# One paired comparison for both one-hots of the gate matrices, and the routing's selection product moved to VectorE

## Chip, core and metric

The kernel runs on one core of a Trainium2 chip. The metric is the device time of one execution in microseconds (us); less is better. The kernel before took 4143.04 us in the median of three runs (4133.16 to 4143.84).

## What is computed

Two trunk layers over 768 tokens of width 1024 (512 latent, 256 context), in float32. Layer 0 mixes tokens by a state-space scan, layer 1 by latent attention. After each mixer comes a PEER channel mixer, and the change lies in it alone:

```python
def peer_route(t, w_q, keys):                      # 8 heads, 128 keys a side, 16 kept
    q = (t @ w_q).reshape(n_tok, 8, 2, 64)
    s = einsum('thsd,hsnd->thsn', q, keys)
    sv, si = lax.top_k(s, 16)                      # per side: scores and key numbers
    cand = sv[:, :, 0, :, None] + sv[:, :, 1, None, :]
    cv, ci = lax.top_k(cand.reshape(n_tok, 8, 256), 16)
    i1 = take_along_axis(si[:, :, 0], ci // 16, -1)
    i2 = take_along_axis(si[:, :, 1], ci % 16, -1)
    return i1 * 128 + i2, softmax(cv)              # 128 experts a token of 16384, their gates

def peer_channel(h, ...):
    act = gelu(einsum('td,tkd->tk', hb, u_tab[ib])) * gb
    return einsum('tk,tkd->td', act, v_tab[ib])
```

## The kernel before, in words

**Tiles of tokens.** Six tiles of 128 tokens: 0 and 1 are context, 2 to 5 latent. In layer 0 tiles 2 to 5 are dense (every one of the 16384 experts is computed for them, and a token's gates, spread over all experts, are zero where an expert was not chosen) and tiles 0 and 1 are gathered (their experts' rows are fetched one by one by indirect DMA). In layer 1, which needs the latent tokens only, tiles 4, 2, 3 are dense and tile 5 is gathered.

**Routing** (`route`, L958, ten tiles in all: six in layer 0, four in layer 1). PE multiplies queries by keys (L984), ACT copies the scores (L987), and VectorE finds the 16 best per head and side (`top16`, L970 to L976), then the 16 best sums (L1010), then the gates (L1014 to L1019) and the positions a and b of the two halves (L1024 to L1034). The key numbers are picked by a selection product: L1039 compares 0..15 with the position into `oh`, 128x2048 in bf16, on VectorE, once per side; L1041 multiplies it by the key numbers `sib` on GpSimd; L1044 (three halvings) and L1045 add it up on VectorE into `rt`.

**Gate matrices** (`gate_matrix`, L1056, seven dense tiles in all). PE turns `rt` (L1064), ACT copies it to `iT` (L1066) and keeps a negated copy (L1067). Then come 16 steps of eight tokens, the one-hots three steps (`GA`) ahead of the products. In `one_hots`, VectorE compares 0..127 with the second keys of eight tokens at once (L1077, `o2`, 128x1024 in f32); `o1`, the one-hot of the first key times the gate, is made token by token: five of eight on VectorE (L1083, comparison and product in one instruction), three of eight (`NACT`) on ACT by two ACTIVATEs each (L1087 and L1088). In `products`, PE makes eight 128x128 float32 products (L1099) and ACT moves four of them at a time from PSUM into `stage` (L1101), whose writes hop by 32 elements. After four steps ACT's queue stores `stage`, 2 MB, to DRAM (L1103). There are 112 such steps, 64 in layer 0 and 48 in layer 1.

**Dense experts.** `dense_u` (L1134) multiplies tokens by 128 experts' u rows with weights split in two float32r parts (split at L305 on ACT and L306 on VectorE or GpSimd). The first 40 blocks of 128 in layer 0 and 48 in layer 1 are made ahead of the gates (`ahead`, L1140, their split on GpSimd) and parked in DRAM. `dense` (L1156) loads the gates `Gt` (on SP's queue, behind the last store of gates), multiplies, and accumulates over v rows (L1204). `gather` (L1257) runs beside: GpSimd issues the row fetches (L1272), VectorE makes the dot products (L1279) and sums (L1284).

**What sets the order.** `merge` emits several streams side by side by a clock of expected times; in `peer` (L1315) the gate matrices and the blocks ahead are the main streams and the gathering is at the side. Then a scheduler orders each engine's instructions by readiness in its own model of costs and hands out buffers. Twenty 4 KB slots (`N4`) per partition are shared by `o1`, `o2`, `oh`, the parts of u and others; `c5` slots are 512 bytes.

Of the kernel before, what the change touches and what calls it, by code (L numbers as in the profile page):

```python
# [35 lines left out]
# Slots of SBUF, by size, that all phases share.  # L36
# [4 lines left out]
NACT = 3  # L41
# [23 lines left out]
def merge(*streams, side=()):  # L65
    """Emits generators side by side; each yields the time its last step takes, or is expected to take. Ends with the
    first ones; those at the side can go on later."""
    clocks = [[0.0, n, s, n < len(streams)] for n, s in enumerate(streams + tuple(side))]
    while any(c[3] for c in clocks):
        c = min(clocks, key=lambda c: (c[0], c[1]))  # L70
        try:
            c[0] += next(c[2])
        except StopIteration:
            clocks.remove(c)
# [12 lines left out]
def pipeline(steps, ahead):  # L87
    """Emits (prepare, work) pairs, with the preparations so many steps ahead of the work."""
    got = []
    for n in range(len(steps) + ahead):  # L90
        if n < len(steps):
            got.append(steps[n][0]())
        if n >= ahead:
            yield steps[n - ahead][1](got[n - ahead])
            got[n - ahead] = None
# [12 lines left out]
class Net:  # L108
    def __init__(self, ctx, tc, a, out, dbg=None):
# [9 lines left out]
        self.iota128 = self.sb.tile([128, 128], F32, name="iota128")  # L119
# [9 lines left out]
    def phase(self, name):  # L129
        """The 48 KB that each phase cuts up as it needs."""  # L130
        self.phases.close()
        self.pool = self.phases.enter_context(self.tc.tile_pool(name=name, bufs=1, reuse_waits="tile"))
# [53 lines left out]
    def ada(self, l, q):  # L186
        """Modulation vectors 2q and 2q+1 of layer l: rows to DRAM, columns to modT."""
# [39 lines left out]
    def adas(self, lqs):  # L227
        """The modulation vectors of several (layer, q); the last part of each runs some steps behind."""
# [12 lines left out]
    def rstd(self, var, eps):  # L241
        """1/sqrt(var + eps) for a [128, 1] operand, with one Newton step."""
# [36 lines left out]
    def transpose_to(self, dst, src, nblk):  # L279
        """dst [128, nblk, 128] <- src [128, nblk*128] transposed by 128-column blocks."""  # L280
# [8 lines left out]
    def mod_transpose(self, h, l, s, i):  # L289
        """[128, 8, 128] <- (h * (1 + mod i+1) + mod i) transposed."""  # L290
# [12 lines left out]
    def split(self, hi, lo, x, lo_eng):  # L303
        """x = hi + lo exactly, both in float32r."""
# [27 lines left out]
    def sin_acc(self, out, x, shift):  # L332
        """sin(x + shift), shift 0 or pi/2, with the argument reduced to [-pi, pi]."""
# [15 lines left out]
    def s5_params(self):  # L349
        """Powers 0..8 of the discrete poles, f * B, and the 8th powers in the scan's layout."""  # L350
        nc, a, par = self.nc, self.a, self.par
        V, GP = nc.vector, nc.gpsimd
        # State before each chunk, [chunk, re/im, (direction, group pair)].
# [4 lines left out]
        # Selects one group of a pair, for both halves of the partitions.  # L358
# [17 lines left out]
        # c of both groups of a pair, by direction, with zeros for the other group's states.  # L376
# [53 lines left out]
        # The 8th and 16th powers as products need them: [state's part, result's part, (direction, group pair)].  # L430
# [15 lines left out]
        # The powers 1..8 again, for both groups of a pair, on both halves of the partitions.  # L446
# [17 lines left out]
    def s5_input(self):  # L464
        """Modulates u, [(j, c), g, chunk], in place."""
# [19 lines left out]
    def s5_advance(self, E, to, of, n, dg, nd):  # L485
        """Adds a step of eight tokens from chunk `of` to chunk `to`, and n - 1 times again for every second chunk on, for nd
        (direction, group pair) from dg."""
# [12 lines left out]
    def s5_prep(self):  # L500
        """Per batch of four (direction, group pair): the chunks' inputs to the states, lag kernels."""
# [7 lines left out]
        def krons(b):  # L509
            """Q, whose rows j are f B times the powers 7 - j forward, j backward."""  # L510
# [14 lines left out]
        def turn(b, Q):  # L525
# [10 lines left out]
            # Lag kernels of both groups of the pairs.  # L536
# [63 lines left out]
    def s5_mout(self):  # L600
        """What the states add to the outputs, [(re/im, state), direction and group pair, group of the pair, (j, c)]:
        rows j are c times the powers j + 1 forward, 8 - j backward."""
# [28 lines left out]
    def s5_scan(self):  # L631
        """The states, [(group of the pair, state), chunk, re/im, direction and group pair], in place; chunks that are done
        are turned to [(re/im, state), chunk, group of the pair, ...]."""
# [26 lines left out]
    def s5_fill(self, fb):  # L660
        """The states between, of four group pairs, both directions; then turned to [(re/im, state), chunk, group of the
        pair, ...]."""
# [10 lines left out]
    def s5_readout(self, mout):  # L673
        """gelu(y + d u), transposed: yc [128, 4, 256] x 2 for the context, yl [128, 2, 512] x 4."""
# [60 lines left out]
    def load_w(self, src, name, n=D):  # L735
        """[D, n] weight as eight tiles [128, n]."""
# [7 lines left out]
    def y_tile(self, ti, k):  # L744
        """Feature block k of tile ti's s5 output, transposed."""
# [5 lines left out]
    def glu(self, ti, wg):  # L751
        """y <- y * sigmoid(y w), in place."""
# [18 lines left out]
    def out_steps(self, l, pair, src, parts, first, rows):  # L771
        """Steps of h <- LN(ALPHA h + m2 * (y w)) for two tiles; parts() gives y's two parts, transposed, as four tiles
        [128, part, block, token]."""
# [134 lines left out]
    def query_steps(self, l, pair, H):  # L908
        """Steps to the PEER layer's input of two tiles, transposed, in two parts, in H; for gathered ones in rows; and to
        the queries, transposed."""  # L910
# [47 lines left out]
    def route(self, ti):  # L958
        """Routes one tile of 128 tokens: its gates and experts, spread over all experts (dense) or listed."""
# [32 lines left out]
        sib = self.c5([128, 2, 8, 16], "sib", BF16)  # L992
        V.tensor_copy(out=sib, in_=si)
        # Candidate pairs (a, b) in the order of 16 a + b, of which those with (a + 1)(b + 1) > 16 can't be among the 16
        # best: row 0 whole, eight of each of rows 1 to 7, the first of rows 8 to 15.
# [16 lines left out]
        # gates  # L1012
# [7 lines left out]
        # position -> (a, b)  # L1020
# [17 lines left out]
        for s in range(2):  # L1038
            V.tensor_tensor(out=oh[s], in0=self.iota16.unsqueeze(1).to_broadcast(full),  # L1039
                            in1=ab[:, s, :].rearrange("p (h k) -> p h k", h=8).unsqueeze(2).to_broadcast(full), op=ALU.is_equal)  # L1040
            GP.tensor_tensor(out=oh[s], in0=oh[s], in1=sib[:, s].unsqueeze(3).to_broadcast(full), op=ALU.mult)  # L1041
        for s in range(2):
# [13 lines left out]
    def gate_matrix(self, ti, n_act=NACT):  # L1056
        """Writes tile di's gates, spread over all experts, to DRAM: [i1 / 8, i2, tile, token / 32, i1 % 8, token % 32]."""
# [7 lines left out]
        iT = self.t2([128, 4, 128], "iT")  # L1065
        S.copy(out=iT[:, 0:3], in_=tp)  # L1066
        S.mul(out=iT[:, 3], in_=tp[:, 0], mul=-1.0)  # L1067
# [3 lines left out]
        def one_hots(q):  # L1071
            """Of eight tokens: the second keys, and the first ones times the gates."""
            t0 = q * 8
            ts = slice(t0, t0 + 8)
            sh = [128, 8, 128]
            o2 = self.t4(sh, "o2")
            V.tensor_tensor(out=o2, in0=self.iota128.unsqueeze(1).to_broadcast(sh),  # L1077
                            in1=iT[:, 1, ts].unsqueeze(2).to_broadcast(sh), op=ALU.is_equal)
            o1 = self.t4(sh, "o1")
            nv = 8 - n_act  # L1080
            for t in range(nv):
                E = GP if t < NPOOL else V
                E.tensor_scalar(out=o1[:, t, :], in0=self.iota128, scalar1=iT[:, 0, t0 + t:t0 + t + 1],  # L1083
                                scalar2=iT[:, 2, t0 + t:t0 + t + 1], op0=ALU.is_equal, op1=ALU.mult)
            for t in range(nv, 8):
                c = t0 + t
                S.activation(out=o1[:, t, :], in_=self.iota128, func=AF.Abs, bias=iT[:, 3, c:c + 1])  # L1087
                S.activation(out=o1[:, t, :], in_=o1[:, t, :], func=AF.Relu, scale=-2.0, bias=iT[:, 2, c:c + 1])  # L1088
            return o1, o2

        def products(q, o):
# [4 lines left out]
            for t4 in range(2):  # L1096
# [4 lines left out]
                S.copy(out=stage[:, :, c:c + 4].rearrange("p i t -> p t i"), in_=gp)  # L1101
# [7 lines left out]
    def gate_matrices(self, n_tiles):  # L1109
        """Of all dense tiles, once the queries of so many tiles are there."""  # L1110
# [14 lines left out]
    def dense_u(self, Us):  # L1125
        """gelu(h u) of 128 experts, [expert, token]."""
# [13 lines left out]
    def ahead(self, l, n, n_tiles):  # L1140
        """The first n blocks' gelu(h u), to DRAM, for use when the gates are there."""
# [14 lines left out]
    def dense(self, l):  # L1156
        """All experts for the tokens of the dense tiles, in blocks of 128 experts; eight blocks to an accumulation."""
# [61 lines left out]
        def work_tile(d):  # L1219
            """The second half of one tile's last accumulation."""  # L1220
# [36 lines left out]
    def gather(self, l, row_time):  # L1257
        """The experts of the other tiles' tokens, row by row."""
# [43 lines left out]
    def peer_out(self, l, ti, f, rows=None):  # L1302
        """h <- LN(ALPHA h + m5 f)."""
# [30 lines left out]
    def mla(self, dense, gather):  # L1334
# [96 lines left out]
        def project(h):  # L1431
            if h % 2 == 0:
# [10 lines left out]
                # Each head's two parts, the first where the head was, the second on the other half of the partitions.  # L1443
# [21 lines left out]
        def scores(h, qi):  # L1465
            """Softmax of one head's scores for 128 queries."""
# [86 lines left out]
def layouts(inputs):  # L1553
    """The inputs as the kernel reads them: copies, transposes and slices only, and tables of shapes alone."""
# [65 lines left out]
```

## Time and profile before

| | us |
|---|---|
| median of three runs | 4143.04 |
| all three | 4143.84, 4143.04, 4133.16 |
| time of the profiled execution | 4133.16 |
| its span | 4133.2 |
| PE busy in it | 3683.9 |
| DVE (VectorE) busy | 3320.3 |
| ACT (ScalarE) busy | 1661.6 |
| POOL (GpSimd) busy | 1716.7 |

The profiled execution is the fastest of the three; its span is its whole time, and the median lies 9.9 us above it. Busy times are sums of one engine's instructions, idle time taken out. A share over the whole span mixes the stages: it is read by stretches below.

### The profile page before, as it was taken

The page shows a single profiled execution, that of the slowest core. Times are in us where ns is not written, and L with a number is a line of the kernel's source. Part 1 is how long each engine was busy: PE and PEld are TensorE (multiplying, and loading weights), DVE is VectorE, ACT ScalarE, POOL GpSimd, SP SyncE. Part 2 cuts the span into 40 slices and gives each one's busy share as a digit, 9 for nine tenths or more (in the row PEclk, how much of TensorE's full clock was granted, in tenths as well). Part 3 has the DMA queues.
Part 4 walks back from the last instruction along what each step waited for, and adds up shares of the span by engine and source line. Part 5 has one row for each costly group of instructions (what it writes and reads, how often), then busy time and mean ns, then how long its engine had stood idle before and what let it go on. Part 6 is the DMA issues. An engine that isn't in the chain of part 4 may idle for free. (4 is left out here: it accounts for less than half of the span.)

```text
span 4133.2 us, 54988 instructions
## 1 busy us (share of the span) xinstructions
PE 3683.9 (89%) x18795; PEld 3040.0 (74%) x18795; DVE 3320.3 (80%) x6733; ACT 1661.6 (40%) x3133; POOL 1716.7 (42%) x1160
## 2 busy tenths in 40 slices
PE   6758968688789999999999989988778899999998
PEld 3437857577667788778888855568778678989997
DVE  9884497999967788988889844468999678888887
ACT  2222335368922232233333233354579333333333
POOL 5834257345422455555555300056445113333341
PEclk7879989899999999999999999999889999999999
DMA  5556234258898799999999820144358878897976
GB/s 180 152 170 228 84 112 148 74 194 273 282 344 301 278 340 344 339 347 340 332 339 346 321 101 3 44 158 134 122 192 271 308 268 316 294 337 278 346 287 219
DMA packets 398457, 986.21 MB, mean 239 GB/s; under 512 B 67040, under 2 KB 147424, under 8 KB 393568
## 3 DMA queue, kind: packets, MB, share of 16 engines
q1 hardware_dynamic: 217120, 501.34, 34.8%
q0 software_dynamic: 110592, 402.70, 27.6%
q10 hardware_dynamic: 70464, 78.65, 5.6%
q8 instruction: 148, 2.42, 0.2%
q14 instruction: 133, 1.09, 0.1%
HBM read 892.28 MB, written 90.21 MB: 238 GB/s over the span
## 5 line engine op out<-in xcount | busy, mean ns | idle before, releaser
L1204 PE MATMUL acc<-Ws,A 128*128 128x512 f32 x5208 | 1204.4, 392 | 54.0 <-ACT A L305 26.5
L1134 PE MATMUL s_ps<-Hs,Uh 128*128 128x512 f32 (+1 forms) x4096 | 1188.9, 371 | 9.6 <-ACT Uh L305 8.7
L1204 PEld LDWEIGHTS acc<-Ws,A 128*128 128x128 f32 x5208 | 982.6, 189 | 271.5 <-DVE Ws L306 35.7
L1272 POOL DMA_INDIRECT row<-in_peer_u,idx x384 | 515.2, 1342 | 823.7 <-DVE row L1279 688.6
L1134 PEld LDWEIGHTS s_ps<-Hs,Uh 128*128 128x128 f32 x4096 | 764.2, 191 | 104.0 <-ACT Uh L305 9.8
L1134 PE MATMUL s_ps<-Hs,Ul 128*128 128x512 f32 (+1 forms) x2048 | 760.7, 371 | 55.8 <-POOL Ul L306 55.7
L1272 POOL DMA_INDIRECT row<-in_peer_v,idx x384 | 479.8, 1250 | 553.8 <-DVE f L1284 489.3
L1284 DVE SCALAR_TENSOR_TENSOR f<-row,act,f 128x1024 f32<-128x1024 f32 x381 | 487.7, 1280 | 39.1 <-DMA row<-in_peer_v,idx 37.7
L1279 DVE SCALAR_TENSOR_TENSOR row<-row,m 128x1024 f32<-128x1024 f32 x384 | 467.1, 1234 | 47.7 <-DMA row<-in_peer_u,idx 46.7
L305 ACT CAST Ws<-W 128x512 fp32r<-128x512 f32 x512 | 306.0, 619 | 495.8 <-DMA W<-in_peer_v 437.0
L1134 PEld LDWEIGHTS s_ps<-Hs,Ul 128*128 128x128 f32 x2048 | 390.4, 191 | 109.3 <-POOL Ul L306 62.6
L306 DVE TENSOR_TENSOR Ws<-W,Ws 128x512 fp32r<-128x512 f32 x512 | 346.2, 686 | 107.8 <-ACT Ws L305 107.3
L305 ACT CAST Uh<-U 128x1024 fp32r<-128x1024 f32 x256 | 268.7, 1052 | 317.9 <-DMA U<-in_peer_uT 257.5
L1137 ACT ACTIVATE ge<-s_ps 128x512 f32<-128x512 f32 (+1 forms) x256 | 139.5, 545 | 454.2 <-PE s_ps L1134 415.9
L306 POOL TENSOR_TENSOR Ul<-U,Uh 128x1024 fp32r<-128x1024 f32 x88 | 228.3, 2596 | 217.0 <-ACT Uh L305 193.8
L1099 PE MATMUL g_ps<-o,o 128*128 128x128 f32 x1792 | 236.0, 289 | 89.6 <-DVE o L1083 75.5
L1099 PEld LDWEIGHTS g_ps<-o,o 128*128 128x128 f32 x1792 | 226.0, 201 | 100.5 <-DVE o L1083 34.1
L306 POOL TENSOR_TENSOR Wos<-wo,Wos 128x512 fp32r<-128x512 f32 x60 | 87.5, 1484 | 472.3 <-PE tp_ps L286 351.2
L305 ACT CAST A<-ge 128x512 fp32r<-128x512 f32 (+1 forms) x256 | 144.6, 565 | 294.7 <-DVE ge L1185 290.5
L1101 ACT COPY stage<-g_ps 128x512 f32<-128x512 f32 x224 | 229.2, 1091 | 55.6 <-PE g_ps L1099 55.1
L306 DVE TENSOR_TENSOR Ul<-U,Uh 128x1024 fp32r<-128x1024 f32 x168 | 205.1, 1221 | 42.2 <-ACT Uh L305 41.4
L1185 DVE TENSOR_TENSOR ge<-ge,Gt 128x512 f32<-128x512 f32 (+1 forms) x256 | 155.9, 620 | 78.1 <-ACT ge L1137 50.6
(346 smaller groups left out, 4927.3 us busy)
## 6 DMA issues: line engine op xcount, KB each, us to landing
U<-in_peer_uT SPq DMA_DIRECT2D x256, 512.0 KB
W<-in_peer_v SPq DMA_DIRECT2D x512, 256.0 KB
gm<-stage ACTq DMA_DIRECT2D x28, 2048.0 KB
ada_wt<-in_ada_w SPq DMA_DIRECT2D x96, 512.0 KB
Gt<-gm SPq DMA_DIRECT2D x16, 2048.0 KB
Gt<-gm SPq DMA_DIRECT2D x16, 1536.0 KB
wq<-in_peer_w_q SPq DMA_DIRECT2D x40, 512.0 KB
wo<-in_s_w_o SPq DMA_DIRECT2D x48, 256.0 KB
```

The costliest lines, as they stand in the source:

```text
L305: self.nc.scalar.copy(out=hi, in_=x)
L306: lo_eng.tensor_tensor(out=lo, in0=x, in1=hi.bitcast(F32), op=ALU.subtract)
L1099: PE.matmul(out=gp[:, t, :], lhsT=o[1][:, t4 * 4 + t, :], rhs=o[0][:, t4 * 4 + t, :], start=True, stop=True)
L1101: S.copy(out=stage[:, :, c:c + 4].rearrange("p i t -> p t i"), in_=gp)
L1134: PE.matmul(out=sp, lhsT=x[:, k, :], rhs=self.Hs[:, y, k, :], start=(n == 0), stop=(n == 3 * KD - 1))
L1137: S.activation(out=ge, in_=sp, func=AF.Gelu)
L1185: V.tensor_tensor(out=gv, in0=gv, in1=Gt[b // SB][:, :, :, b % SB, :], op=ALU.mult)
L1204: PE.matmul(out=acc[hf][d], lhsT=A[b][:, x, c], rhs=Ws[:, y], start=(j == 0 and n == 0), stop=(j == SB - 1 and n == 2))
L1272: GP.indirect_dma_start(out=r, out_offset=None, in_=tab, in_offset=bass.IndirectOffsetOnAxis(ap=ik[:, k:k + 1], axis=0), element_offset=l ...
L1279: x = V.scalar_tensor_tensor(out=r, in0=r, scalar=1.0, in1=m, op0=ALU.mult, op1=ALU.mult, accum_out=act[:, k:k + 1])
L1284: x = V.scalar_tensor_tensor(out=f, in0=r, scalar=act[:, k:k + 1], in1=f, op0=ALU.mult, op1=ALU.add)
```

## The change

`iota128` becomes bf16. The key numbers of a tile are kept in bf16, each written twice in a row (`iT`), with both sides of eight tokens next to each other, and one comparison of 128x2048 in bf16 gives both one-hots. ACT copies the second one to f32 (`o2`). The first is multiplied by the gates: six of eight tokens in one VectorE instruction, two (`NACT = 2`) on ACT, one instruction each. In the routing, `sib` is kept doubled as well, one tile per side, and the selection product is VectorE's. The move out of PSUM writes `stage` in runs of four and hops in what it reads.

```diff
-NACT = 3
+NACT = 2
-        self.iota128 = self.sb.tile([128, 128], F32, name="iota128")
+        self.iota128 = self.sb.tile([128, 128], BF16, name="iota128")
...
-        sib = self.c5([128, 2, 8, 16], "sib", BF16)
-        V.tensor_copy(out=sib, in_=si)
+        sib = [self.c5([128, 128, 2], f"sib{s}", BF16) for s in range(2)]
+        for s in range(2):
+            V.tensor_copy(out=sib[s], in_=si[:, s].rearrange("p h k -> p (h k)").unsqueeze(2).to_broadcast([128, 128, 2]))
...
-            GP.tensor_tensor(out=oh[s], in0=oh[s], in1=sib[:, s].unsqueeze(3).to_broadcast(full), op=ALU.mult)
-        for s in range(2):
+            o = oh[s].rearrange("p h a (k x) -> p (h a) k x", x=2)
+            V.tensor_tensor(out=o, in0=o, in1=sib[s].unsqueeze(2).to_broadcast([128, 128, 8, 2]), op=ALU.mult)
...
-        iT = self.t2([128, 4, 128], "iT")
-        S.copy(out=iT[:, 0:3], in_=tp)
-        S.mul(out=iT[:, 3], in_=tp[:, 0], mul=-1.0)
+        iT = self.t2([128, 16, 2, 8, 2], "iT", BF16)
+        for x in range(2):
+            S.copy(out=iT[:, :, x], in_=tp[:, 1 - x].rearrange("p (q t) -> p q t", t=8).unsqueeze(3).to_broadcast([128, 16, 8, 2]))
+        gT = self.c5([128, 128], "gT")
+        S.copy(out=gT, in_=tp[:, 2])
...
-            o2 = self.t4(sh, "o2")
-            V.tensor_tensor(out=o2, in0=self.iota128.unsqueeze(1).to_broadcast(sh),
-                            in1=iT[:, 1, ts].unsqueeze(2).to_broadcast(sh), op=ALU.is_equal)
-            o1 = self.t4(sh, "o1")
+            e = self.t4([128, 2, 8, 128], "e", BF16)
+            V.tensor_tensor(out=e.rearrange("p s t (i x) -> p (s t) i x", x=2),
+                            in0=self.iota128.rearrange("p (i x) -> p i x", x=2).unsqueeze(1).to_broadcast([128, 16, 64, 2]),
+                            in1=iT[:, q].rearrange("p s t x -> p (s t) x").unsqueeze(2).to_broadcast([128, 16, 64, 2]),
+                            op=ALU.is_equal)
+            o2 = self.t4([128, 8, 128], "o2")
+            S.copy(out=o2, in_=e[:, 0])
+            o1 = self.t4([128, 8, 128], "o1")
             nv = 8 - n_act
-            for t in range(nv):
-                E = GP if t < NPOOL else V
-                E.tensor_scalar(out=o1[:, t, :], in0=self.iota128, scalar1=iT[:, 0, t0 + t:t0 + t + 1],
-                                scalar2=iT[:, 2, t0 + t:t0 + t + 1], op0=ALU.is_equal, op1=ALU.mult)
+            V.tensor_tensor(out=o1[:, 0:nv], in0=e[:, 1, 0:nv],
+                            in1=gT[:, t0:t0 + nv].unsqueeze(2).to_broadcast([128, nv, 128]), op=ALU.mult)
             for t in range(nv, 8):
-                c = t0 + t
-                S.activation(out=o1[:, t, :], in_=self.iota128, func=AF.Abs, bias=iT[:, 3, c:c + 1])
-                S.activation(out=o1[:, t, :], in_=o1[:, t, :], func=AF.Relu, scale=-2.0, bias=iT[:, 2, c:c + 1])
+                S.mul(out=o1[:, t, :], in_=e[:, 1, t, :], mul=gT[:, t0 + t:t0 + t + 1])
...
-                S.copy(out=stage[:, :, c:c + 4].rearrange("p i t -> p t i"), in_=gp)
+                S.copy(out=stage[:, :, c:c + 4], in_=gp.rearrange("p t i -> p i t"))
```

## Rows read from the trace of the kernel before

**Rows 1.** The page: engines over the span, then busy tenths in 40 slices.

```profile
PE 3683.9 (89%) x18795; PEld 3040.0 (74%) x18795; DVE 3320.3 (80%) x6733; ACT 1661.6 (40%) x3133; POOL 1716.7 (42%) x1160
...
DVE  9884497999967788988889844468999678888887
```

**Rows 2.** Engines by stretch, dense part of layer 0, columns as in rows 3.

```profile
1900.00:2300.00 400.00, 400.00 (x1743) 326.95 (x1742) 356.13 (x455) 120.48 (x181) 220.80 (x172) 1.00 0.95 346
```

**Rows 3.** The same view, routing and gates by layer; columns in the first line.

```profile
core 0: us, PE busy (x) PEld busy (x) DVE busy (x) ACT busy (x) POOL busy (x), PEclk, DMA share, GB/s
487.00:870.00 383.00, 297.02 (x1743) 253.65 (x1741) 350.17 (x1421) 149.80 (x254) 194.37 (x87) 0.89 0.32 104
870.00:1138.00 268.00, 225.21 (x1381) 199.67 (x1382) 251.16 (x484) 236.81 (x508) 135.95 (x76) 0.94 0.83 273
2830.00:3010.00 180.00, 142.00 (x833) 134.15 (x833) 169.52 (x703) 76.76 (x135) 90.17 (x36) 0.90 0.39 122
3010.00:3210.00 200.00, 165.86 (x1110) 162.35 (x1110) 183.52 (x321) 175.84 (x366) 103.22 (x51) 0.92 0.74 243
```

**Rows 4.** Chain that ended last, end of layer 1's gates: start, us, what.

```profile
3202.89 6.91 ACT stage L1101 x7
3209.82 14.44 DMA gm<-stage
```

**Rows 5.** VectorE in order of time, one undisturbed step: start us, us, what.

```profile
774.10 1.22 DVE L1077 TENSOR_TENSOR o<-iota,iT 128x1024 f32<-128x1024 f32 x1
775.23 1.37 DVE L1083 TENSOR_SCALAR o<-iota,iT 128x128 f32<-128x128 f32 x5
776.51 1.22 DVE L1077 TENSOR_TENSOR o<-iota,iT 128x1024 f32<-128x1024 f32 x1
```

**Rows 6.** Groups, 870 to 1138: busy us, mean ns | idle before.

```profile
L1083 DVE TENSOR_SCALAR o<-iota,iT 128x128 f32<-128x128 f32 x300 | 107.0, 434 | 0.0
L1077 DVE TENSOR_TENSOR o<-iota,iT 128x1024 f32<-128x1024 f32 x60 | 84.1, 1401 | 12.8 <-ACT iT L1066 10.0 <-issue 2.8
...
L1101 ACT COPY stage<-g_ps 128x512 f32<-128x512 f32 x121 | 123.2, 1087 | 15.3 <-PE g_ps L1099 15.3
...
L1087 ACT ACTIVATE o<-iota,iT 128x128 f32<-128x128 f32 x174 | 61.9, 394 | 8.2 <-DVE rt L1045 4.6 <-issue 2.3 <-DVE o L1083 1.3
L305 ACT CAST Uh<-U 128x1024 fp32r<-128x1024 f32 x17 | 18.2, 1069 | 0.7 <-ACT o L1088 0.6
```

**Rows 7.** Instructions on tile o by stretch (PE, PEld, DVE, ACT busy).

```profile
870.00:1138.00 268.00, 128.45 (x960) 121.92 (x960) 184.85 (x360) 110.88 (x348) 0.94 0.83 273
...
3010.00:3210.00 200.00, 79.28 (x633) 76.87 (x632) 129.51 (x234) 73.75 (x234) 0.92 0.74 243
```

**Rows 8.** One line's instructions: ns min/median/max, first and last start us, forms.

```profile
L1039 DVE TENSOR_TENSOR oh<-iota,ab x20: 1174/1219/4549, 520.0 to 3014.1; 128x2048 bf16<-128x2048 bf16 x20
...
L1041 POOL TENSOR_TENSOR oh<-oh,sib x20: 3631/3646/4692, 521.4 to 3018.6; 128x2048 bf16<-128x2048 bf16 x20
```

**Rows 9.** A plain move of 128x512 out of PSUM, routing of layer 0.

```profile
L987 ACT COPY scr<-sp 128x512 f32<-128x512 f32 x24 | 13.0, 590 | 5.3 <-PE sp L984 2.5 <-POOL wq L306 2.3 <-ACT ge L1137 0.4
```

**Rows 10.** Instructions on tile oh, the four stretches summed (DVE, POOL).

```profile
sum 1031.00, DVE 141.99 POOL 79.12; mean DVE 35.50 POOL 19.78
```

**Rows 11.** Timeline: selection products, VectorE beside; then groups of adds, 870 to 1138.

```profile
758.45 8.14 POOL L1041 TENSOR_TENSOR oh<-oh,sib 128x2048 bf16<-128x2048 bf16 x2 [2.45 <-DVE oh L1039]
...
763.03 4.57 DVE L1044 TENSOR_TENSOR oh<-oh 128x1024 bf16<-128x1024 bf16 x2 [3.53 <-POOL oh L1041]
...
L1044 DVE TENSOR_TENSOR oh<-oh 128x512 bf16<-128x512 bf16 x2 | 0.8, 420 | 0.0
L1044 DVE TENSOR_TENSOR oh<-oh 128x1024 bf16<-128x1024 bf16 x1 | 0.7, 685 | 0.0
L1044 DVE TENSOR_TENSOR oh<-oh 128x256 bf16<-128x256 bf16 x2 | 0.6, 292 | 0.1
```

**Rows 12.** Waits, 487 to 755: us in total, times, longest.

```profile
DVE rw L972 <- ACT scr L987: 28.8, 2, 26.8
```

More of the change, by code (lines that the diff above doesn't have):

```diff
@@ L1073, in one_hots @@
             t0 = q * 8
-            ts = slice(t0, t0 + 8)
-            sh = [128, 8, 128]
-            o2 = self.t4(sh, "o2")
-            V.tensor_tensor(out=o2, in0=self.iota128.unsqueeze(1).to_broadcast(sh),
-                            in1=iT[:, 1, ts].unsqueeze(2).to_broadcast(sh), op=ALU.is_equal)
-            o1 = self.t4(sh, "o1")
+            e = self.t4([128, 2, 8, 128], "e", BF16)
[6 more added lines that the diff above has]
+            o1 = self.t4([128, 8, 128], "o1")
             nv = 8 - n_act
-            for t in range(nv):
-                E = GP if t < NPOOL else V
-                E.tensor_scalar(out=o1[:, t, :], in0=self.iota128, scalar1=iT[:, 0, t0 + t:t0 + t + 1],
-                                scalar2=iT[:, 2, t0 + t:t0 + t + 1], op0=ALU.is_equal, op1=ALU.mult)
+            V.tensor_tensor(out=o1[:, 0:nv], in0=e[:, 1, 0:nv],
+                            in1=gT[:, t0:t0 + nv].unsqueeze(2).to_broadcast([128, nv, 128]), op=ALU.mult)
             for t in range(nv, 8):
-                c = t0 + t
-                S.activation(out=o1[:, t, :], in_=self.iota128, func=AF.Abs, bias=iT[:, 3, c:c + 1])
-                S.activation(out=o1[:, t, :], in_=o1[:, t, :], func=AF.Relu, scale=-2.0, bias=iT[:, 2, c:c + 1])
+                S.mul(out=o1[:, t, :], in_=e[:, 1, t, :], mul=gT[:, t0 + t:t0 + t + 1])
             return o1, o2
```

## The prediction

> **What bounds the kernel now.** I read first the page's engines and slices [rows 1]: VectorE (DVE) is busy 80% of the span, PE 89%, and no engine is full everywhere, so the stage decides. Next the engines by stretch. In the dense part of layer 0 PE is busy without a gap [rows 2] and the change issues nothing in either layer's dense part: that time is fixed and can only start earlier. The stretches that the change touches are the four of routing and gates, 1031 us together [rows 3]. There VectorE is busy 350 of 383, 251 of 268, 170 of 180 and 184 of 200 us, 91 to 94%; PE is behind it (78 to 84%) at a granted clock of 0.89 to 0.94, ACT is at 88% in both stretches of gates. So VectorE is the first bound, and PE and ACT stand close behind it. Last I followed the chain that ended last over the end of layer 1's gates [rows 4]: seven moves of ACT into stage, the store of 14.44 us, and then the loads that the dense part begins with. Nothing hides that end: what the gates end earlier, the dense part begins earlier.
>
> **The gate steps.** One undisturbed step of eight tokens takes VectorE 2.41 us, from 774.10 to 776.51: 1.13 us to the first token's instruction, 0.26 us for each of five [rows 5]. The stretch of layer 0's gates spent 184.85 us on 60 steps, 3.08 each [rows 6, 7]; the mean token there takes 434 ns [rows 6], and the 0.67 us above 2.41 are waits inside the instructions, which I leave as they are.
> After: one comparison of 2048 bf16 columns and one product of 768 columns into f32. The routing's comparison of 2048 bf16 columns takes 1174 ns at the least [rows 8]; I take 1.17 us. The other end is two such comparisons as o2's in f32, 2.44 us [rows 5]. I choose 1.17 since the routing's has the same type, length and engine and also repeats one input, in rows of 16. The product is 768/1024 of o2's 1.13 us with its fixed part whole: 0.87 us. Sum 2.04 in place of 2.41 us, 0.37 saved, over 112 steps **41 us**.
>
> **ACT** loses per step three pairs of ACTIVATEs, 6 x 0.39 = 2.36 us, and gains a copy of 1024 columns, 1.07 us as for Uh [rows 6], and two products, 0.78 us. It also moves PSUM twice per step at 1.09 us [rows 6]; a plain move of the same size takes 0.59 us [rows 9]. The new move writes runs and hops in what it reads; no row shows ACT hopping in PSUM, so it costs between 0.59 and 1.09, and a little above if reading hops worse. I take 0.59: a plain move also reads PSUM, and the known cost belongs to the hopping write that goes. ACT's step falls from 4.54 to 3.0 us (4.0 at the other end), so its share of a stretch falls and it hides under VectorE. It counts only at the two ends, where seven moves stand alone [rows 4]: 7 x 0.5 = 3.5 us per layer, **7 us**. What is new is that PE's weights, o2, now come through ACT's queue; whoever waits there waits for PE's own moves too, and three steps of lead cover a late copy by some 9 us. The turned gates cost one copy more per tile, 7 x 0.3 = **2 us** lost.
> The paired tile e takes a third 4 KB slot per step from the twenty. It is held until ACT's copy has run; what could be late next are the loads of u ahead. I give this nothing in the sum, as ACT has room, and keep it as a case.
>
> **The routing.** VectorE's instructions on oh take 142.0 us [rows 10]. By their shortest or undisturbed durations they need 20 x 1.17 for the comparisons [rows 8] and 20 x (0.69 + 0.42 + 0.29 + 0.29) for the adds [rows 11], 57 us; 85 us are waits inside them. GpSimd's twenty products ran 79.1 us in the same stretches [rows 10], and one case shows what that does: while the products run from 758.45 to 766.6, two adds of 0.69 us take 4.57 together, after 3.53 us idle [rows 11]. The products go, and with them between 0 and 79 of those 85 us; other GpSimd work holds VectorE too, as in the gate steps, so I take 60, and 10 more for ten such idle waits, most of which other work fills. VectorE gains twenty products of 2048 bf16 columns at 1.17 and ten more casts of 0.3: 26 us. Net **44 us** saved (from 26 lost to 63 saved). GpSimd is freed of 79 us; behind its products stood the splits of the u blocks and of the output weights, so those come earlier as well.
>
> **The sum.** 41 + 44 = 85 us of VectorE's time, of a bound that is busy 93%. Not all arrives. In the first stretch VectorE waits 26.8 us at once for scores of queries that are not there yet [rows 12], and PE, busy 225 of 268 us in layer 0's gates, has room for 43 us at most [rows 3]. I let 0.8 through: 68 us. With 7 and less 2: **73 us**. The profiled execution, 4133.2 us with nothing around its span, would take 4060; the median stands 9.9 us above it, so the forecast for the median is 4143 - 73 = **4070 us**.
>
> **Where a page says otherwise.** Row 5's comparison repeats one 4-byte key 128 times and still passes one column per cycle, so repeating costs nothing there, and I expect the same of a repeated pair. The Trainium skill (Vector Engine (DVE) Microarchitecture Reference, Measured stream behaviour on trn2) has a port at full rate only for runs of two adjacent 4-byte words, and 1.73 ns per column otherwise; a pair of bf16 is one word. By that figure, an estimate, the comparison would take 1.85 us and the sum would be about zero. No row here has a repeated pair.
>
> **Rivals.**
> *The pair does not run at two columns per cycle* (the change does not do what it says; slower). A hop costs (1087 - 590)/512 = 0.97 ns on ACT [rows 6, 9]; for 1024 fetches of pairs that makes the comparison 2.17 us. Then a gate step takes 3.04, 112 x 0.63 = 71 us more, and the routing saves 70 - 20 x 2.17 - 3 = 24: 47 more, 38 at 0.8, **4181 us**. It decides from 1.81 us on, where 112(c + 0.87 - 2.41) + 20c + 3 = 70. Against it: the routing's comparison [rows 8] and the repeated f32 key [rows 5]. The page's rule above is this rival at its mildest. Chance 0.10.
> *PE or the queries hold half of it.* PE runs 78 to 84% of these stretches [rows 3] and half its clock is not granted at times; the four engines would have to overlap better than now. With half the factor, 0.4 x 85 = 34, less 2: **4111 us**, 4095 to 4130. For it: rows 12 and ACT's 88%. Against: a denser PE is granted more clock, as in the dense part [rows 2]. Chance 0.17.
> *Slots or ACT's queue eat the gain*: e keeps ACT's copy on the way from VectorE to PE, steps go at 4.47 us as now (268/60), and only the moves' 7 us remain: **4136 us**, about the same. Against: ACT's work per step falls. Chance 0.06.
> *All arrives and GpSimd's waits shrink too* (the 0.67 us per step): 85 + 5 + 25: **4030 us**. Chance 0.06.
>
> **How the numbers follow.** The forecast has 0.61, its own range 4040 to 4095 (factor 0.6 to 1, the move out of PSUM at either end). A measurement can tell about 0.3%, 12 us. Faster by more: 0.61 + 0.17 + 0.06 = 0.84; the same 0.06; slower 0.10. The range leaves out the slower rival, the one that eats the gain, and part of the fastest: 4025 to 4130.
>
> **What would show it.** Right: the comparison of e near 1.2 us, the product near 0.9; adds on oh mostly 0.3 to 0.7 and no product on GpSimd; ACT's moves near 0.6; the last store of gates some 40 us earlier in layer 0 and the dense parts as long as before. Wrong: e above 1.8; PE's products waiting on ACT's o2 where they now wait on VectorE; the stretches as long with VectorE idle; or a dense part that has grown.

## The result, and the profile after

The changed kernel takes **4077.85 us** in the median (4075.69 to 4081.01); the kernel before took 4138.9 in the four runs beside it. The ratio is 0.985, 95% interval 0.9838 to 0.9863: 61 us less. The forecast was 73 us less, 4070, within 4025 to 4130. The profiled execution took 4075.69 us, with a span of 4073.6.

The page, engines over the span and VectorE's busy tenths, which answer to [rows 1]:

```profile
PE 3664.2 (90%) x18795; PEld 3029.0 (74%) x18795; DVE 3231.9 (79%) x6315; ACT 1558.1 (38%) x2804; POOL 1638.1 (40%) x1140
...
DVE  8784498988877788988888844469987678888887
```

VectorE lost 88 us of busy time, ACT 104, GpSimd 79, and PE 20 (the same matmuls; the mean granted clock of the profiled execution was 0.947 and is 0.953). Now the four stretches of [rows 3], cut at the same events: the routing of layer 0, its gates, and both again in layer 1.

```profile
core 0: us, PE busy (x) PEld busy (x) DVE busy (x) ACT busy (x) POOL busy (x), PEclk, DMA share, GB/s
487.00:840.00 353.00, 289.57 (x1726) 247.44 (x1725) 327.13 (x1421) 141.04 (x228) 149.68 (x75) 0.92 0.34 112
840.00:1097.00 257.00, 217.79 (x1397) 195.15 (x1396) 224.76 (x243) 187.47 (x348) 128.37 (x72) 0.96 0.85 283
2797.00:2952.00 155.00, 130.37 (x748) 123.23 (x749) 144.17 (x649) 66.17 (x104) 63.00 (x29) 0.90 0.42 135
2952.00:3153.00 201.00, 172.51 (x1161) 169.53 (x1160) 165.66 (x194) 140.58 (x255) 98.21 (x48) 0.94 0.73 243
```

The routing got shorter by 30 and 25 us (383 to 353, 180 to 155), the gates by 11 in layer 0 and not at all in layer 1 (268 to 257, 200 to 201). Yet it is the gates' engines that emptied: VectorE is busy 166 us of layer 1's 201, and was 184 of 200. The forecast had put the two parts about equal.

Single instructions after. First VectorE in order of time over one undisturbed step (start us, us, what), to be held against [rows 5]; between two steps there is a dot product of the gathering. From start to start, as in [rows 5], the step takes 2.19 us (1017.80 to 1019.99), 1.31 to the product's start and 0.88 from there:

```profile
1017.80 1.21 DVE L1080 TENSOR_TENSOR e<-iota,iT 128x2048 bf16<-128x2048 bf16 x1
1019.11 0.96 DVE L1088 TENSOR_TENSOR o<-e,gT 128x768 f32<-128x768 bf16 x1
1019.99 1.22 DVE L1282 SCALAR_TENSOR_TENSOR row<-row,m 128x1024 f32<-128x1024 f32 x1
```

Then groups of layer 0's gates, 840 to 1097, as [rows 6]:

```profile
L1102 PE MATMUL g_ps<-o,o 128*128 128x128 f32 x992 | 127.6, 288 | 39.2 <-ACT o L1085 24.8 <-DVE o L1088 14.4
...
L1080 DVE TENSOR_TENSOR e<-iota,iT 128x2048 bf16<-128x2048 bf16 x60 | 79.7, 1329 | 17.2 <-ACT iT L1070 17.2
L1104 ACT COPY stage<-g_ps 128x512 f32<-128x512 f32 x124 | 68.4, 583 | 12.8 <-PE g_ps L1102 12.4
...
L1085 ACT CAST o<-e 128x1024 f32<-128x1024 bf16 x60 | 62.9, 1049 | 25.3 <-DVE e L1080 23.6 <-ACT ge L1140 1.2
```

The move out of PSUM is at 583 ns, where it took 1087. And PE's idle time before the products, which was VectorE's in the kernel before, is now mostly ACT's: 24.8 us for the copy o2. For comparison the kernel before, 870 to 1138 (us in total, times, longest):

```profile
PE g_ps L1099 <- DVE o L1083: 32.1, 16, 7.5
```

Last the routing's instructions on oh (ns min/median/max, first and last start), then their busy time over the four stretches, as [rows 8, 10]:

```profile
L1041 DVE TENSOR_TENSOR oh<-iota,ab x20: 1171/1218/3443, 522.2 to 2963.9; 128x2048 bf16<-128x2048 bf16 x20
L1044 DVE TENSOR_TENSOR oh<-oh,sib x20: 1171/1216/3443, 523.5 to 2965.4; 128x2048 bf16<-128x2048 bf16 x20
...
sum 966.00, DVE 111.02; mean DVE 27.76
```

With twenty more products on it, VectorE spends 111 us on oh in place of 142. Gone too is the time that it sat idle for GpSimd's product, in the kernel before (us, times):

```profile
  POOL oh L1041: 16.5, 5
```

### The profile page after: what moved, and what is told of

Its sections match the earlier page's. It is cut to its first block, busy times and chain, and to the rows that moved or that the text cites. A ratio compares the mean times of both kernels' runs of the same rounds, so it can differ in the third digit from the quotient of the medians.

```text
span 4073.6 us, 54069 instructions
## 1 busy us (share of the span) xinstructions
PE 3664.2 (90%) x18795; PEld 3029.0 (74%) x18795; DVE 3231.9 (79%) x6315; ACT 1558.1 (38%) x2804; POOL 1638.1 (40%) x1140
## 4 chain that ended last, share of the span: by engine, by line
PE 45%; issue 10%; DVE 10%; DMA 5%; POOL 5%; ACT 3%; ACTq 0%; POOLq 0%; DVEq 0%; SPq 0%
PE s_ps L1137 20%; PE acc L1207 15%; POOL row L1275 4%; PE g_ps L1102 3%; DMA row<-in_peer_v,idx 2%; DMA W<-in_peer_v 1%; DVE row L1282 1%; PE op_mla L1507 1%; DMA ge<-ged 1%; DVE e L1080 1%; DVE Ws L306 1%; PE acc L1228 1%; DVE f L1287 1%; PE kvp L1365 1%; ACT o L1085 1%
## 5 line engine op out<-in xcount | busy, mean ns | idle before, releaser
L1282 DVE SCALAR_TENSOR_TENSOR row<-row,m 128x1024 f32<-128x1024 f32 x384 | 490.4, 1293 | 54.7 <-DMA row<-in_peer_u,idx 53.8
L306 DVE TENSOR_TENSOR A<-ge,A 128x512 fp32r<-128x512 f32 (+1 forms) x256 | 158.4, 620 | 45.6 <-ACT A L305 44.7
```

Of the source, the lines that this page charges most:

```text
L306: lo_eng.tensor_tensor(out=lo, in0=x, in1=hi.bitcast(F32), op=ALU.subtract)
L1282: x = V.scalar_tensor_tensor(out=r, in0=r, scalar=1.0, in1=m, op0=ALU.mult, op1=ALU.mult, accum_out=act[:, k:k + 1])
```

## The experiments

Each was timed beside the kernel before (4138 to 4141 us); ratios are to that.

### The two parts alone

In the first, the routing's lines are as before (undone); in the second, they alone are changed:

```diff
-            V.tensor_tensor(out=o, in0=o, in1=sib[s].unsqueeze(2).to_broadcast([128, 128, 8, 2]), op=ALU.mult)
+            GP.tensor_tensor(out=oh[s], in0=oh[s], in1=sib[:, s].unsqueeze(3).to_broadcast(full), op=ALU.mult)
```

> The changed kernel with the selection product of the routing back on GpSimd, and the small cast as before: the gates' part of the change alone. By the sum of the prediction the gates bring 41 x 0.8 = 33 us, 7 at the ends and lose 2: 38 us off 4139, so 4101 us. The rival that the trace of the changed kernel suggests: after the last route the gates end only 11 us sooner in layer 0 and no sooner in layer 1, so the gates alone bring some 10 to 15 us: 4125 to 4130 us, and nearly all of the gain is the routing's.

> The kernel before with the selection product alone moved to VectorE: the routing's part alone. By the sum of the prediction 44 x 0.8 = 35 us off 4139: 4104 us. By the rival (the routes of layer 0 end 30 us and those of layer 1 another 25 us sooner in the changed kernel, gates beside them included) some 45 to 50 us: about 4090 us. If the two parts were independent, this gain and that of the gates alone would add up to 61 us.

Measured: the gates' part alone 4129.11 us, ratio 0.9976 (0.9967 to 0.9985), 11.5 us gained; the routing's part alone 4088.0 us, 0.9875 (0.986 to 0.989), 52.6 us gained. Together 64 against the 61 of the whole change: they add up. The prediction had 38 and 35.

### What GpSimd's product cost

GpSimd does the twenty products again, on tiles that nobody reads any more:

```diff
+            GP.tensor_tensor(out=oh[s], in0=oh[s],
+                             in1=sib[s].rearrange("p (h k) x -> p h k x", h=8)[:, :, :, 0:1].to_broadcast(full), op=ALU.mult)
```

> The changed kernel, and GpSimd does the same twenty products again on the tile after VectorE has read its last sum, so nobody waits for a result; only the old load on GpSimd comes back. If the cost of the old product was that VectorE's instructions wait while GpSimd works (60 of the 85 us in the prediction), most of it returns: 0.8 x 60 = 48 us on 4078, 4126 us. If the cost was the dependency (VectorE waiting for the product to be ready) or VectorE's place in the order, nothing returns beyond GpSimd's later splits: 4078 to 4088 us.

Measured: 4138.65 us, ratio 1.0002 (0.9992 to 1.0012). The whole gain of the change is gone, though nobody reads these products (the trace has 0.8 us of waiting for them in all). The page of this run:

```profile
PE 3676.9 (89%) x18795; PEld 3038.1 (73%) x18795; DVE 3285.1 (79%) x6315; ACT 1558.5 (38%) x2804; POOL 1721.8 (42%) x1160
```

VectorE has the same 6315 instructions in the same order as in the changed kernel and is busy 53 us longer. Its timeline shows how; a stretch beside one product, then one beside two:

```profile
531.70 0.30 DVE L972 MAX8 rw<-scr 128x8 f32<-128x128 f32 x1
531.76 3.67 POOL L1048 TENSOR_TENSOR oh<-oh,sib 128x2048 bf16<-128x2048 bf16 x1 [49.79 <-DVE rt L1047]
531.90 3.68 DVE L1047 TENSOR_TENSOR rt<-oh 128x128 f32<-128x128 bf16 x1
...
535.58 0.28 DVE L973 FIND_INDEX8 rw<-rw,scr 128x8 uint32<-128x128 f32 x1
535.78 3.77 DVE L1055 SCALAR_TENSOR_TENSOR idx<-rt 128x128 int32<-128x128 f32 x1
...
721.14 7.33 POOL L1048 TENSOR_TENSOR oh<-oh,sib 128x2048 bf16<-128x2048 bf16 x2 [4.78 <-DVE rt L1047]
...
721.64 0.28 DVE L973 FIND_INDEX8 rw<-rw,scr 128x8 uint32<-128x128 f32 x1
721.84 0.07 DVE L974 MATCH_VALUE_LOAD tk_tmp<-rw,scr 128x8 f32 x1
721.90 0.27 DVE L974 MATCH_REPLACE8 tk_tmp<-rw,scr 128x128 f32<-128x128 f32 x1
```

An add of 128 columns (0.28 us elsewhere) takes 3.68 us, as long as the product beside it. Between 721 and 728 the searches for the best 16 run on at 0.27 us with two products beside them. The Trainium skill (SBUF — State Buffer, SBUF: two separate sides) has one port pair that VectorE and GpSimd lock for a whole instruction, taken on VectorE's side by, among others, an instruction with two inputs from SBUF; the trace agrees for the add (3.68 us) and for the index (3.77 us), which have two inputs. MAX8, with one, goes free. So do FIND_INDEX8 and MATCH_REPLACE8, for which the profile names two tiles; whether they read both is not shown here. GpSimd is busy 84 us longer as well, and the splits behind the products come later; this run does not part the two. Nor are the products where they were: here they come behind the last sum and fall beside the gates' one-hots and the index, while in the kernel before they fell beside the adds on oh.

### The move out of PSUM

The old move in the changed kernel, and then the new move alone in the kernel before:

```diff
-                S.copy(out=stage[:, :, c:c + 4], in_=gp.rearrange("p t i -> p i t"))
+                S.copy(out=stage[:, :, c:c + 4].rearrange("p i t -> p t i"), in_=gp)
```

> The changed kernel with the old move out of PSUM, which writes to stage in hops of 32 words and reads PSUM in runs. By the prediction only the two ends pay: 7 moves x 0.5 us in each layer, 7 us, so 4085 us. The rival: the products of the gates now wait for ACT's copy of the second one-hot, 25 us in layer 0's gates, and 0.5 us more in each of 224 moves stands ahead of those copies in the same queue: 20 to 40 us more, 4098 to 4118 us. If PE's wait is not due to ACT at all, less than 3 us.

> The kernel before with nothing changed but the move out of PSUM: it writes stage in runs and hops in what it reads. The gates' part of the change brought 11.5 us alone, and the old move put back into the changed kernel cost 26. Theory 1, the move is worth as much here: 26 us off 4139, 4113 us, and then the new one-hots themselves cost some 14 us. Theory 2, the move counts only where PE's weights come through ACT's queue, as in the changed kernel: here PE waited for VectorE, so only the two ends gain, 4 to 7 us: 4132 to 4135 us.

Measured: 4103.75 us with the old move in the changed kernel, 0.9917 (0.9903 to 0.993), 26 us more than the changed kernel. The new move alone in the kernel before: 4126.75 us, 0.9972 (0.9963 to 0.9982), 11 us gained, between the two theories. In both pairs PE, VectorE, ACT and GpSimd have their instructions in the same order, so that these are the prices of the longer moves alone. The move matters more once o2 passes through ACT: PE's waits for o2, 24.8 us in the changed kernel, are 31.6 with the old move, and those of its weight loads 53.8 (44.3). From the waits of that run, 840 to 1110 (us in total, times, longest):

```profile
PEld g_ps L1102 <- ACT o L1085: 53.8, 26, 7.5
...
PE g_ps L1102 <- ACT o L1085: 31.6, 22, 4.4
```

### The old one-hots

The changed kernel with the one-hots of before (five tokens on VectorE in f32, three on ACT); routing and move stay changed.

```diff
-            V.tensor_tensor(out=o1[:, 0:nv], in0=e[:, 1, 0:nv],
-                            in1=gT[:, t0:t0 + nv].unsqueeze(2).to_broadcast([128, nv, 128]), op=ALU.mult)
+            for t in range(nv):
+                E = GP if t < NPOOL else V
+                E.tensor_scalar(out=o1[:, t, :], in0=self.iota128, scalar1=iT[:, 0, t0 + t:t0 + t + 1],
+                                scalar2=iT[:, 2, t0 + t:t0 + t + 1], op0=ALU.is_equal, op1=ALU.mult)
...
```

> The changed kernel with the one-hots of the kernel before (f32, five tokens with VectorE, three with ACT), while the selection product stays on VectorE and the move stays the new one. Theory 1 (the move is worth 26 us with either kind of one-hots, the new one-hots cost): 4139 - 53 - 26 = 4060 us, faster than the changed kernel by some 15. Theory 2 (the move is worth only the ends here): 4139 - 53 - 6 = 4080 us, the same as the changed kernel, and the one-hots bring their gain only because the move makes room on ACT.

Measured: 4079.2 us, 0.9868 (0.9853 to 0.9884), the same as the changed kernel: theory 2. With the runs above this makes a square, all four with the new routing:

| us | old move | new move |
|---|---|---|
| old one-hots | 4088.0 | 4079.2 |
| new one-hots | 4103.75 | 4077.85 |

The new one-hots cost 16 us with the old move and bring 1 with the new one, less than this can tell from nothing. The window 850 to 1090 of both kernels says that VectorE's time was freed all the same; first the old one-hots, then the changed kernel:

```profile
850.00:1090.00 240.00, 203.32 (x1303) 182.57 (x1302) 240.00 (x446) 185.59 (x496) 126.65 (x69) 0.96 0.87 289
```

```profile
850.00:1090.00 240.00, 202.82 (x1300) 181.70 (x1299) 208.00 (x216) 177.50 (x330) 122.97 (x68) 0.96 0.87 291
```

VectorE is busy 240 of 240 us with the old one-hots and 208 with the new, and PE gets through the same matmuls in both (1303 and 1300). The 32 us are there and nobody uses them.

### The pair

Each key once in iT; the comparison repeats a single bf16 element.

```diff
-        iT = self.t2([128, 16, 2, 8, 2], "iT", BF16)
+        iT = self.t2([128, 16, 2, 8], "iT", BF16)
...
-                            in1=iT[:, q].rearrange("p s t x -> p (s t) x").unsqueeze(2).to_broadcast([128, 16, 64, 2]),
+                            in1=iT[:, q].rearrange("p s t -> p (s t)").unsqueeze(2).to_broadcast([128, 16, 128]),
```

> The changed kernel with each key once in iT, so that the comparison repeats one bf16 element 128 times and no pair. If it is the pair that lets VectorE pass two columns per cycle, the comparison takes 2.2 to 2.4 us in place of 1.2, 112 us more of VectorE in all; at the prediction's 0.8 that is 90 us: 4168 us; where the gates have room on VectorE, 30 to 60: 4108 to 4138 us. If one repeated element runs as fast as a pair, nothing changes: 4078 us.

Measured: 4175.98 us, 1.0095 (1.0081 to 1.011), 98 us more than the changed kernel, slower than the kernel before. The comparison:

```profile
L1080 DVE TENSOR_TENSOR e<-iota,iT x112: 2265/2285/4486, 745.5 to 3236.1; 128x2048 bf16<-128x2048 bf16 x112
```

2.285 us in place of 1.218, 120 us over 112 steps, of which 98 reach the end: 0.8 of each us. The routing's product keeps its pair in this run. So VectorE does pace the gates when it gets slower; when it gets faster, something else takes over.

### What takes over

Two candidates show in the waits: VectorE idles for the next tile's keys, 17.2 us in layer 0 (above), and PE for o2. First, the steps of one tile run on into the next:

```diff
-            yield from self.gate_matrix(ti)
+            for prep, work in self.gate_matrix(ti):
+                ahead.append((work, prep()))
+                if len(ahead) > GA:
+                    work, o = ahead.pop(0)
+                    yield work(o)
...
+        for work, o in ahead:
+            yield work(o)
```

> The changed kernel, and the gate steps of one tile run on into the next: the transposes and turned keys of the next tile are issued with its first one-hots, three steps ahead of their products, and not after the last product of the tile before. In the changed kernel VectorE idles 17 us in layer 0's and 25 us in layer 1's gates for those keys. If VectorE's one-hots set the pace of the gates, some 20 to 35 us go: 4043 to 4058 us. If PE or ACT sets it, less than 10: 4068 to 4078 us.

Measured: 4055.37 us, 0.9799 (0.9786 to 0.9811), 22 us below the changed kernel. Nearly all of it comes in layer 1, where the last move starts at 3132.2 us and not at 3152.6; in layer 0 it is at 1095.3 and was at 1096.1. Waits of this run in layer 0, 850 to 1090, VectorE's and then PE's:

```profile
DVE o L1088 <- PE s_ps L1150: 20.1, 8, 4.2
DVE e L1080 <- ACT iT L1070: 3.9, 2, 2.1
...
PE g_ps L1102 <- ACT o L1085: 34.9, 32, 2.2
```

The wait for keys went from 17.2 to 3.9 us, and another grew from 3.9 to 20.1: the product of VectorE into o1 waits until PE has finished a block of u. The reading is that o1 is to take this block's 4 KB slot; the run with slots tests it. The same edit with the old one-hots:

> The kernel with the old f32 one-hots, the new move and the selection product on VectorE (4079 us, as fast as the changed kernel at 4078), and the gate steps of one tile run on into the next, as in the joined version of the changed kernel (4055 us). It asks where the gain of the new one-hots went. If VectorE sets the pace with the old ones (it is busy 240 of 240 us there) and only the drain between tiles hid what the new ones save, joining brings little here: 4070 to 4079 us, 15 to 24 slower than the joined version with the new one-hots. If the new one-hots save nothing that counts (PE's wait for ACT's copy and for slots takes it all), joining brings the same 23 us: 4053 to 4059 us.

Measured: 4077.07 us, 0.986 (0.9845 to 0.9875): joining brings 2 us there. VectorE is full, and stays so:

```profile
850.00:1090.00 240.00, 203.74 (x1284) 181.42 (x1283) 240.00 (x438) 184.38 (x494) 124.59 (x67) 0.97 0.86 283
```

So with the drain between tiles out of the way the new one-hots are worth 22 us (4077 to 4055); with it, nothing. Then the slots: e in two of its own, eighteen for the rest.

```diff
-N4 = 20
+N4 = 18
...
-            e = self.t4([128, 2, 8, 128], "e", BF16)
+            e = self.sm([128, 2, 8, 128], "e", BF16)
```

> The joined version of the changed kernel, and e no longer takes its slots from the twenty of 4 KB: it has two of its own, and the others are eighteen. In the joined version VectorE idles 20 us in layer 0's gates for slots that PE's blocks of u hold. If the slots are what the new one-hots give their gain back to, 10 to 25 us go: 4030 to 4045 us. If ACT's copy alone is late, or eighteen slots hold back the loads of u, no gain or a loss: 4055 to 4065 us.

Measured: **4021.76 us**, 0.971 (0.9695 to 0.9725), 34 us below the joined version and 56 below the changed kernel. Window and waits (VectorE's, then PE's), 850 to 1090:

```profile
850.00:1090.00 240.00, 222.16 (x1423) 199.14 (x1421) 228.56 (x241) 180.43 (x343) 139.08 (x80) 0.98 0.94 322
```

```profile
DVE row L1295 <- DMA row<-in_peer_u,idx: 7.2, 5, 2.9
DVE e L1080 <- ACT iT L1070: 3.3, 2, 2.7
...
PE g_ps L1102 <- DVE o L1088: 12.0, 9, 3.2
PE g_ps L1102 <- ACT stage L1104: 3.4, 2, 2.3
PE g_ps L1102 <- ACT o L1085: 1.3, 1, 1.3
```

VectorE's wait for slots is gone, PE's wait for o2 fell from 34.9 to 1.3 us, and PE does 1423 matmuls in the same 240 us. VectorE, at 229, is near its bound again. The last move of layer 0 starts 21 us earlier (1074.2), the rest of the gain comes in layer 1 (3098.3).

The edit does two things at once. It ends the wait for slots, and the scheduler, with slots free, makes another order of instructions. Counted over layer 0's gates, the copy of o2 stands in ACT's queue 1.6 steps ahead of the moves in the joined version, 2.0 in the changed kernel and 3.4 here. What ACT's copy waited for, in the joined version and then here (850 to 1090; 59 and 58 copies):

```profile
ACT o L1085 <- DVE e L1080: 12.5, 2, 10.3
```

```profile
ACT o L1085 <- DVE e L1080: 34.6, 25, 3.5
```

In the joined version the copy hardly ever waits for e: e is ready long before, and the copy stands behind moves that wait for PE (one e ends at 1049.48, its copy starts at 1053.85). Here the copy is often at the head of the queue before e is done. So the 34 us belong to the slots; how much of them is VectorE's wait and how much the place of the copy in ACT's queue is not parted. Slots of its own for e without the joining were not run.

A step more of lead on top of that (`GA = 4`):

> The version with two slots of its own for e, and the one-hots are made four steps ahead of their products in place of three. If PE waits for o2 because ACT's copy comes late behind moves that wait for PE (22 to 35 us in layer 0's gates), a step more of lead takes 10 to 20 us of that away: 15 us below the version with three. If the pace is set elsewhere (VectorE's own sum, or two more slots of eighteen that are held), the same within 5 us, or slower by 5 to 10.

Measured: 4024.49 us, 0.9729 (0.9715 to 0.9742): no gain; the wait that a longer lead would cover had gone already (1.3 us). Last, o2 without ACT:

```diff
...
-            S.copy(out=o2, in_=e[:, 0])
+            for s, r in ((0, o2), (1, e[:, 1])):
+                V.tensor_tensor(out=r.rearrange("p t (i x) -> p t i x", x=2),
+                                in0=self.iota128.rearrange("p (i x) -> p i x", x=2).unsqueeze(1).to_broadcast([128, 8, 64, 2]),
+                                in1=iT[:, q, s].unsqueeze(2).to_broadcast([128, 8, 64, 2]), op=ALU.is_equal)
```

> The changed kernel, but the second one-hot goes straight from VectorE's comparison into f32, with no copy on ACT: VectorE makes two comparisons of 1024 columns in place of one of 2048. VectorE pays 1.13 + 0.6 in place of 1.21 us, 0.5 us more in each of 112 steps, 58 us; ACT is freed of 1.05 us per step, and PE's weights no longer come through its queue. If PE's wait for ACT's copy is what took the gain of the gates, the time stays or falls in spite of VectorE: 4065 to 4080 us. If VectorE sets the pace, 0.8 x 58 = 46 us more: 4124 us; in between, both share it.

Measured: 4101.61 us, 0.991 (0.9895 to 0.9925), 24 us more than the changed kernel, in between: 0.68 us more per step (1.22 + 0.68 in place of 1.22), 77 us over 112 steps, and 0.3 of it arrives, in exchange for ACT's copy. PE's wait for ACT is gone, and one for VectorE stands in its place, 850 to 1090:

```profile
PE g_ps L1101 <- DVE o L1087: 41.0, 16, 7.4
```

## Why the prediction was right in the sum and wrong in its parts

**The prices of instructions held; the sum of a step did not.** The pair runs at the rate of the routing's comparison: e takes 1.22 us (1.17 foreseen). By the rule that the prediction takes from the Trainium skill (Vector Engine (DVE) Microarchitecture Reference, Measured stream behaviour on trn2), an estimate, it would have been 1.85. The measurement decides: the page's 1.73 ns is its row for one source that hops at every element, and a repeated pair does not pay it. The rival in which the pair fails stood at 4181 us for 2.17 (it left out the 7 and 2 us of the main sum; with them it is 4176); the run with single keys had 2.285 and 4176, but there e alone lost its pair, and the rival had the routing's products lose it too. The copy o2 took 1.05 (1.07), the move 0.586 (0.59), the product 0.88 from start to start (0.87).

The sum of a step took e's 1.17 by its length and the other terms from start to start. Behind its own comparison the product starts 0.10 us after e's end, so e costs 1.31; the step takes 2.19 us and not 2.04 and saves 0.22, 25 us and not 41. In the version with slots, in another order of instructions, the same two take 1.13 and 0.87, the 2.0 that was foreseen:

```profile
1006.72 1.21 DVE L1080 TENSOR_TENSOR e<-iota,iT 128x2048 bf16<-128x2048 bf16 x1
1007.85 0.94 DVE L1088 TENSOR_TENSOR o<-e,gT 128x768 f32<-128x768 bf16 x1
1008.72 3.55 DVE L1295 SCALAR_TENSOR_TENSOR row<-row,m 128x1024 f32<-128x1024 f32 x1
```

**The step that failed is the common factor: "Not all arrives ... I let 0.8 through", on both parts alike.** One factor was set for all of VectorE's time, from a busy share of 93% and two rows on waits. It has no such single value:

- **Routing, 35 foreseen, 52.6 measured.** On oh VectorE's time came out as foreseen: 142.0 busy and 16.5 idle for the product, less 111.0 and less 3 for the casts, is 44.5 us, with 44 in the sum. About all of it arrived, and not 0.8: the medians have 8 us more, the two profiled executions 3 less (4133.16 to 4091.52). Where 8 more would come from is not shown. They are not in VectorE's other instructions: in the run of the routing alone its busy time fell by 18 us in all, less than on oh. GpSimd was freed of 67 us, and in layer 1's routing PE's waits for its splits fell from 19.3 to 8.5 us: a candidate that no run tests alone. The page of that run, to be held against [rows 1], then these waits, in the kernel before (2830 to 3010) and in that run (2805 to 2971):

```profile
PE 3681.1 (90%) x18795; PEld 3040.2 (74%) x18795; DVE 3301.9 (81%) x6763; ACT 1665.8 (41%) x3133; POOL 1649.5 (40%) x1140
```

```profile
PE s_ps L1134 <- POOL Ul L306: 19.3, 9, 8.0
```

```profile
PE s_ps L1135 <- POOL Ul L306: 8.5, 10, 2.1
```

- **One-hots, 25 us of VectorE's time, nothing arrived.** The square of four runs shows it, and VectorE's 32 idle us of 240 with it. A part of each tile is a chain of keys, e, o2 and products that starts only when the tile before has drained; e's third slot makes o1 wait for PE's blocks and, as the run with slots suggests, keeps the copy of o2 close to PE's own moves in ACT's queue. The prediction gave the slot nothing in the sum, "as ACT has room". Of the rivals, *slots or ACT's queue eat the gain* had this, with 0.06, for the whole change; it is true of one part. Slots and drain together were worth 56 us.
- **The move, 7 us foreseen at the ends.** It brings 11 us alone in the kernel before and 26 in the changed one, since it is what makes room on ACT for the copy. In layer 0 the ends gained nothing: the last move starts 40 us earlier (1136.4 to 1096.1), but PE's last product with u only 33 (2343.2 to 2309.8), since PE went on with blocks of u while the old moves ran (from 1130.91, with the last product of the gates done). In layer 1 PE's last product ended at 3152.6 after and the dense part followed, as the chain of the changed kernel shows (start, us, what):

```profile
3150.55 2.05 PE g_ps L1102 x16
3152.60 12.66 PE s_ps L1137 x72
...
3165.75 9.95 DMA Gt<-gm
```

The seven moves of [rows 4] are gone from the chain, and the store of 14.44 us with them; PE's blocks lie there now.

So 4070 against 4078 is one term too small by 18 us and another, the gates' 38, too large by 27. That the two nearly cancel is luck; nothing in the prediction sets one against the other. Two of its smaller sums do not come out either: factor 1 with 7 for the moves and less 2 gives 4053, not the 4040 at which its own range begins, and the 25 us in the rival at 4030 come from no row. The signs of the prediction's own list told it: the last move of layer 0's gates came 40 us earlier, as foreseen, and the dense parts kept their length within 7 us; but PE's products waited on ACT's o2, which stood under "wrong", and the stretch of gates in layer 1 was as long as before with VectorE idle, which stood there too.

## What to carry to other kernels

An engine that is 93% busy is a bound only until the next hand-off. Before its saved time is counted, look at what the consumer waits for at the seams (the first step of each tile, the slot that an added tile takes from a shared pool), and clear those with the change. Here that was worth 56 us, nearly as much as the change itself. An elementwise product on GpSimd beside a busy VectorE can cost VectorE more than doing the product itself: in the run with idle products 53 us of busy time, where twenty products of 1.216 us are 24. The cost can fall on instructions that have nothing to do with the product; put it back with nobody waiting for it, and the cost shows.

## What the runs showed of the hardware that was not expected

- VectorE compares 128x2048 in bf16 with a repeated pair in 1.20 us at the least, with a repeated single element in 2.265 us. The first was the prediction's choice, for which it had no row.
- Beside a GpSimd product of 3.67 us VectorE's add and index wait for as long as it runs (3.68 and 3.77 us); MAX8, FIND_INDEX8 and MATCH_REPLACE8 keep their 0.27 us.
- ACT reads PSUM in hops of 128 words, writing runs of four, at the price of a plain move (0.586 us, against 0.590 in [rows 9]); the move that writes SBUF in hops of 32 words costs 0.5 us more for 512 columns (1.087 in [rows 6]).
